# Seven products of sums in place of eight for the logits and gates of a two-layer mixer

## The chip, the cores and the metric

One core of one Trainium2 chip runs the whole network as one program. TensorE (PE) multiplies, VectorE (DVE), ScalarE (ACT) and GpSimd (POOL) do the element work, and all transfers are issued from SyncE's queue (SP). The metric is the device time of one execution in microseconds (us). The kernel before takes 1518.46 us, the median of three runs (the lowest is 1518.29).

## The reference, cut to what matters

Two layers; 512 latent tokens and 256 context tokens, 1024 channels. In each layer the normalised input h goes through one wide input projection, three branches (retention, gMLP, differential attention) make 512 channels each, and the branches are merged by gates that are sigmoids of further columns of the same projection:

```python
def merge_branches(o_ret, o_mlp, o_diff, merge_logits, w_bo, w_o):
    g_ret, g_mlp, g_diff = jnp.split(jax.nn.sigmoid(merge_logits), N_BRANCH, axis=-1)
    y = g_ret * (o_ret @ w_bo[0]) + g_mlp * (o_mlp @ w_bo[1]) + g_diff * (o_diff @ w_bo[2])
    return y @ w_o

# in each layer, with h the modulated, normalised stream (latents, and in layer 0 the context too):
rk_, rv_, dk_, dv_, rq_, rg_, dq_, dg_, mu_, mv_, mg_, mlog_ = split_cols(h @ w_in[l], IN_SIZES)
o_ret  = from_heads(rms_norm(ret_o)) * jax.nn.silu(rg_)
o_diff = from_heads(rms_norm(diff_o) * (1.0 - lam_init)) * jax.nn.silu(dg_)
o_mlp  = mu_ * spatial_mix(layer_norm(mv_)) * jax.nn.silu(mg_)
out = merge_branches(o_ret, o_mlp, o_diff, mlog_, w_branch_out[l], w_out[l])
```

mlog_ has 3072 columns (1024 for each branch), each of the gates and of mu_, mv_ has 512. All is in float32.

## The kernel before, in words

**Precision.** A float32 product is made of three products in TensorE's reduced type: x = xh + xl and w = wh + wl, and wh·xh + wh·xl + wl·xh is accumulated. xh is a copy by ScalarE into the reduced type, xl is x − xh by VectorE; such a pair of instructions is called a split here (`w_split`, L642, for 512 words of weights at a time; `split_into` for activations). h lies split in SBUF through a whole layer (`HH`, `HL`, eight blocks of 128 channels by up to 768 tokens).

**Weights.** They come from HBM in blocks, in the order of `block_list` (L33), through two raw buffers of 2048 words for each partition, and are split into one of two places (`RING`): while one block is multiplied, the next is split. A logit block `m` holds 128 columns of the logits and 128 columns of the branch's output projection.

**A layer** (`run`, L1775): the projections of attention and retention with both branches' own work woven in; then, for the attention branch, the gate `dg` and the merge `d`; for retention the gate `rg` and the merge `r`; then the gMLP (mv, its layer norm, mg, the position mixing and mu) and the merge `m`; then the output phase with the norm and, in layer 0, the next layer's h. In the gates and merges the weights are TensorE's stationary operand (128 columns) and h streams through: 384 tokens at a time in layer 0 (two spans of 768), 512 in layer 1 (latents alone). For 256 columns that is 2 x 2 x 8 x 3 = 96 matmuls 384 wide in layer 0, and 2 x 8 x 3 = 48 matmuls 512 wide in layer 1. The merge (L1477) adds a logit block and an output block for each 128 channels of y: a sigmoid by ScalarE, a multiplication by VectorE, and an addition to y, by GpSimd in the second merge (`ptt`, L1506) and by VectorE in the third.

**Beside it**, in the merges `r` and `m` of layer 0, VectorE computes the modulation of the next layer and the output gate of this one: 32 rows of `wmod`, each loaded by a transfer into one of two buffers and reduced by one or two `ttr` instructions of 1024 elements (L374, in the profile CUSTOM_DVE_ANT_0 with a short read of its accumulator), 56 in all. They write their unused product into the weights' place (`mjunk`).

**What sets the order.** The program records its operations; each has its priority (its place in the recording, moved by a `bump`). `schedule` (L404) then lays them out by a list of assumed costs (L304 to L401), each engine taking the ready operation of lowest priority number. Its result is only an order: on the chip each engine works through its own queue in that order and waits by semaphores. Nearly every instruction comes from one of a few helper lines: L314 matmuls, L318 transposes, L339 ScalarE, L351 tensor_tensor on VectorE, L374 ttr, L392 tensor_tensor on GpSimd, L401 transfers.

Of the kernel before, what the change touches and what calls it, by code (L numbers as in the profile page):

```python
# [568 lines left out]
NR = 32768  # L569


class Prog:
    def __init__(self, nc, R, AR, AFl, PSM, ap):
# [32 lines left out]
    def F(self, *shape):  # L606
# [843 lines left out]

    def gate(self, l, c):
# [3 lines left out]
        oz = Z if c == "d" else Z + 6144  # L1455
        self.OT = self.arv(Z + 3072, 4, NT), self.arv(Z + 9216, 4, NT)
        for i in range(2):
            self.begin(l, f"{c}g{i}")
            W = self.W(l, f"{c}g{i}")
            for j in range(2):  # L1460
                ch = 2 * i + j
                R.tag = f"L{l}.{c}g{ch}"
# [4 lines left out]
                for v, a, b in self.spans(l):
                    R.act(sg[:, a:b], ps[v].ap, AF.Sigmoid)
                for v, a, b in self.spans(l):
                    R.tt(sg[:, a:b], ps[v].ap, sg[:, a:b], ALU.mult)  # L1470
# [4 lines left out]
                self.step()

    def merge(self, l, c, extra=None):  # L1477
# [9 lines left out]
        for i in range(8):  # L1487
            self.begin(l, f"{c}m{i}")
            R.tag = f"L{l}.{c}m{i}"
            Wl = self.W(l, f"{c}m{i}", 128)  # L1490
            Wb = self.W(l, f"{c}m{i}", 128, 1024, 4)
            ps, pb = self.banks(l), self.banks(l)
            sg = F(n)
            y = self.Y[i]
            dst = y if first else sg
            for v, a, b in reversed(self.spans(l)):
                R.tag = f"L{l}.{c}m{i}"
                self.ws(ps[v].ap, (self.HH, self.HL), slice(a, b), Wl, 0)
                self.ws(pb[v].ap, self.OT, slice(a, b), Wb, 0)
                R.tag += ".ev"  # L1500
                R.act(sg[:, a:b], ps[v].ap, AF.Sigmoid)
                R.tt(dst[:, a:b], pb[v].ap, sg[:, a:b], ALU.mult)
                if last:
                    R.tt(y[:, a:b], y[:, a:b], sg[:, a:b], ALU.add)
                    if v == len(self.spans(l)) - 1:
                        self.y_split(l, 0, i)  # L1506
            if not first and not last:
                R.ptt(y.ap, y.ap, sg.ap, ALU.add)
            sg.free()
            for p in (*ps, *pb):  # L1510
                p.free()
            if extra:
                extra(i)
            self.step()
# [374 lines left out]
```

## Time and profile before

| | us |
|---|---|
| median of three runs | 1518.46 |
| the profiled execution | 1517.34 |
| its span, first to last instruction | 1515.5 |
| PE busy | 1493.6 (99%) |
| DVE busy | 797.2 (53%) |
| ACT busy | 600.3 (40%) |
| POOL busy | 170.4 (11%) |

The profiled execution is 1.8 us longer than its span and 1.1 us below the median. Busy time counts an instruction from its start to its end; instructions of one engine that follow each other overlap by some tens of ns, so a row's mean is longer than the distance from one start to the next, and the distance is what a full queue pays. Lines named "windows" give the busy time of each engine in a stretch of the span.

### The profile page before, as it was taken

Reading aid. Unit: us, or ns where it says so; the run is one execution under the profiler, and the core shown is the slowest. Engines: PE = TensorE matmul, PEld = TensorE weight load, DVE = VectorE, ACT = ScalarE, POOL = GpSimd, SP = SyncE. Lnnn points to the kernel's source line nnn. Section 1 sums busy time; section 2 is a strip of 40 time slices with the busy share of each in tenths; the row PEclk is TensorE's granted clock in tenths of the full one; section 3 lists DMA queues with packets and bytes.
Section 4 is the critical chain, followed back from the end, with each engine's and each line's share of the span. In section 5 each row is a group of like instructions: output and inputs, shape, how many; then the busy total and the mean of one; then the engine's idle time right before and its main releaser. Section 6 shows DMA issues by size and latency. Waiting matters only on the chain.

```text
span 1515.5 us, 22649 instructions
## 1 busy us (share of the span) xinstructions
PE 1493.6 (99%) x9040; PEld 1372.6 (91%) x9040; DVE 797.2 (53%) x1551; ACT 600.3 (40%) x1292; POOL 170.4 (11%) x187
## 2 busy tenths in 40 slices
PE   6999999999999999999999999999999999999998
PEld 4789998999999999999999899989998888888887
DVE  4456646565233962335974664674656334344462
ACT  6635644563222222222223462554455333332341
POOL 1211111210000011001000130111211000201000
PEclk9999999999999999999999999999999999999999
DMA  9351322111231532032663233332211332321331
GB/s 362 137 154 36 87 71 60 57 64 45 86 113 56 177 129 84 29 105 76 193 210 125 84 115 92 118 84 84 84 42 57 117 106 84 125 95 62 122 125 70
DMA packets 37705, 156.25 MB, mean 103 GB/s; under 512 B 5344, under 2 KB 6496, under 8 KB 31200
## 3 DMA queue, kind: packets, MB, share of 16 engines
q1 hardware_dynamic: 37600, 154.81, 30.8%
q8 instruction: 71, 1.16, 0.3%
q14 instruction: 34, 0.28, 0.1%
HBM read 132.77 MB, written 4.19 MB: 90 GB/s over the span
## 4 chain that ended last, share of the span: by engine, by line
PE 94%; DVE 2%; issue 1%; DMA 1%; POOL 1%; ACT 0%; SPq 0%; DVEq 0%; POOLq 0%; ACTq 0%
PE PSM L314 91%; PE PSM L318 3%; POOL AF L392 1%; DVE AR L351 0%; ACT AF L339 0%; DVE AF L351 0%; DMA AF<-AF 0%; SPq L401 0%; DMA AF<-w 0%; DVE AF L360 0%; DVE AF L370 0%; DVE AF L366 0%; ACT AR L339 0%; DVEq L1885 0%; POOLq L1885 0%
## 5 line engine op out<-in xcount | busy, mean ns | idle before, releaser
L314 PE MATMUL PSM<-AR 128*128 128x384 f32 (+2 forms) x7512 | 1354.5, 339 | 0.7 <-DVE AF L351 0.7
L314 PEld LDWEIGHTS PSM<-AR 128*128 128x128 f32 x7512 | 1208.5, 189 | 100.9 <-issue 1.2
L339 ACT ACTIVATE AR<-AF 128x512 fp32r<-128x512 f32 (+4 forms) x489 | 284.4, 606 | 414.4 <-PE PSM L314 274.7
L351 DVE TENSOR_TENSOR AR<-AF,AR 128x512 fp32r<-128x512 f32 (+3 forms) x486 | 316.5, 668 | 231.1 <-ACT AR L339 193.3
L392 POOL TENSOR_TENSOR AF<-AF 128x128 f32<-128x128 f32 (+5 forms) x180 | 169.7, 951 | 1340.0 <-DVE AF L351 533.0
L339 ACT ACTIVATE AF<-PSM 128x256 f32<-128x256 f32 (+5 forms) x379 | 169.9, 467 | 356.4 <-PE PSM L314 321.3
L351 DVE TENSOR_TENSOR AF<-PSM,AF 128x512 f32<-128x512 f32 (+3 forms) x253 | 144.8, 581 | 256.2 <-PE PSM L314 160.4
L314 PE MATMUL PSM<-AF 128*128 128x128 f32 (+3 forms) x1104 | 142.0, 300 | 11.8 <-DMA AF<-wmodn 9.6
L314 PEld LDWEIGHTS PSM<-AF 128*128 128x128 f32 (+1 forms) x1104 | 127.0, 184 | 21.3 <-DVE AF L360 9.4
L339 ACT ACTIVATE AF<-PSM,AF 128x768 f32<-128x768 f32 (+2 forms) x144 | 90.9, 646 | 77.8 <-DVE AF L358 48.3
L370 DVE TENSOR_REDUCE AF<-PSM 128x2 f32<-128x1536 f32 (+1 forms) x40 | 61.6, 1542 | 35.7 <-PE PSM L314 35.6
L374 DVE CUSTOM_DVE_ANT_0 AR<-AF 128x1024 fp32r<-128x1024 f32 x59 | 75.3, 1277 | 6.5 <-DMA AF<-wmod 6.1
L360 DVE TENSOR_SCALAR AF<-AF 128x1 f32<-128x1 f32 (+3 forms) x188 | 42.8, 237 | 56.9 <-ACT AF L339 48.8
L318 PE MATMUL PSM<-AF 128*128 128x128 f32 x424 | 67.7, 277 | 3.2 <-ACT AF L339 3.2
L339 ACT ACTIVATE AF<-AF 128x256 f32<-128x256 f32 (+4 forms) x107 | 54.5, 557 | 32.8 <-POOL AF L392 13.4
L318 PEld LDWEIGHTS PSM<-AF 128*128 128x128 f32 x424 | 51.1, 141 | 14.2 <-ACT AF L339 6.4
L351 DVE TENSOR_TENSOR AF<-AF 128x512 f32<-128x512 f32 (+5 forms) x78 | 43.1, 561 | 14.8 <-POOL AF L392 6.0
L366 DVE SCALAR_TENSOR_TENSOR AF<-AF 128x768 f32<-128x768 f32 (+2 forms) x48 | 42.8, 900 | 3.8 <-POOL AF L392 2.7
L382 DVE BATCH_NORM_STATS2 AF<-AF 128x6 f32<-128x512 f32 x10 | 6.7, 691 | 37.6 <-ACT AF L339 37.5
L366 DVE SCALAR_TENSOR_TENSOR AF<-AF,PSM 128x128 f32<-128x128 f32 x64 | 19.9, 344 | 12.4 <-PE PSM L314 6.1
L358 DVE TENSOR_SCALAR AF<-AF 128x2 f32<-128x2 f32 (+4 forms) x98 | 22.1, 239 | 3.2 <-ACT AF L339 1.7
L360 DVE TENSOR_SCALAR AF<-PSM,AF 128x128 f32<-128x128 f32 x48 | 15.8, 403 | 11.4 <-PE PSM L318 11.4
(20 smaller groups left out, 97.9 us busy)
## 6 DMA issues: line engine op xcount, KB each, us to landing
AF<-w SPq DMA_DIRECT2D x50, 1024.0 KB, 4.8
AF<-w SPq DMA_DIRECT2D x48, 768.0 KB, 4.3
AF<-wmod SPq DMA_DIRECT2D x32, 512.0 KB, 4.1
AF<-wmodn SPq DMA_DIRECT2D x16, 512.0 KB, 8.9
AF<-x SPq DMA_DIRECT2D x12, 512.0 KB, 4.4
AR<-AR SPq DMA_DIRECT2D x16, 384.0 KB, 4.3
AF<-AF SPq DMA_DIRECT2D x64, 64.0 KB, 2.0
AR<-AF SPq DMA_DIRECT2D x12, 256.0 KB, 2.3
```

Source lines behind the costliest of these rows:

```text
L314: self.add("PE", lambda: pe.matmul(out, lhsT, rhs, start=start, stop=stop), [out], [lhsT, rhs], c)
L318: self.add("PE", lambda: pe.transpose(out, in_, ident), [out], [in_, ident], 109.0)
L339: return self.add("ACT", lambda: e.activation(out, in_, func, **kw), outs, ins, c, tab)
L351: return self.add("DVE", lambda: v.tensor_tensor(out, a, b, op=op), [out], [a, b], self.n(out) / 0.97 + 84)
L358: f = lambda: v.tensor_scalar(out, a, s1, None, op0=op0)
L360: f = lambda: v.tensor_scalar(out, a, s1, s2, op0=op0, op1=op1)
L366: return self.add("DVE", lambda: v.scalar_tensor_tensor(out, a, s, b, op0=op0, op1=op1), [out], ins, self.n(out) / 0.97 + 130)
L370: return self.add("DVE", lambda: v.tensor_reduce(out, in_, axis=AX.X, op=op), [out], [in_], self.n(in_) / 0.96 + 72)
L374: return self.add("DVE", lambda: v.tensor_tensor_reduce(junk, a, b, 1.0, 0.0, ALU.mult, ALU.add, accum), [junk, accum], [a, b], self.n(a) ...
L382: return self.add("DVE", lambda: v.bn_stats(out, in_), [out], [in_], self.n(in_) / 0.96 + 72)
L392: return self.add("POOL", lambda: g.tensor_tensor(out, a, b, op=op), [out], [a, b], c)
```

## The change

The 256-column products of the logits (`dl`, `rl`, `ml`, four each) and of the gates are no longer made of eight products of quarters (two halves of the channels, two of the columns, two of the tokens) but of seven products of sums of quarters (`seven`). In layer 0 this holds for the logits, rg, mg and mu, 18 products; in layer 1 for the logits, mg and mu, 16. dg, and rg in layer 1, remain eight (`SEVEN`).

- Four sums of quarters of h are made once in a layer and split (`sums`, `sums_split`): S1 = h10 + h11, S2 = S1 − h00, S3 = h00 − h10, S4 = h01 − S2 (first index the half of the tokens, second the half of the channels). S2 and S1 are split after dg, S3 and S4 after mv, whose weights lie in S3's place.
- Four sums of quarters of the weights are made for each product, in the raw buffer, and each of the seven quarters is split (`p_split`): 512 words, into one of five slots of 1024 words (`NSLOT`), which the quarters and the pieces of the output blocks use in turn. A slot is written again when TensorE has read it.
- Each product of quarters is 4 x 3 = 12 matmuls, 384 wide in layer 0 and 256 in layer 1, into a bank of its own. Eight instructions on the results (a copy by ScalarE and seven additions by VectorE, with PSUM as one input) put the four quarters of the result together in SBUF; the sigmoid then reads SBUF.
- The logits and the output projection have blocks of their own (`l` 2048 words, `b` 1024), so a merge goes through four pairs of 256 columns. y is added up a span at a time.
- mv and the layer norm come right after dg (`mlp_v`); mg, mu and the mixing stay ahead of the third merge. The retention's normalised output goes through a DRAM buffer (`scr2`) and comes back when rg is computed; before it lay in SBUF, where S1 is now. `wo0` and `wo1` change places, and y's first group is split in new places.
- The 56 ttr now start in the merge `d` (`MODS`: 8 rows there, 12 in `r`, 12 in `m`), with a priority number raised by 100, and write their product into the upper half of the second raw buffer.

```diff
-    for g in "dr":
-        out += [(f"{g}g{i}", 2048) for i in range(2)] + [(f"{g}m{n}", 1536) for n in range(8)]
-    out += [(f"mv{i}", 2048) for i in range(2)] + [(f"mg{i}", 2048) for i in range(2)] + [(f"mu{i}", 2048) for i in range(2)]
-    out += [(f"mm{n}", 1536) for n in range(8)]
+    for g in ("dg", "mv", "d", "rg", "r", "mg", "mu", "m"):
+        if len(g) == 2:
+            out += [(f"{g}{i}", 2048) for i in range(2)]
+        else:
+            out += [x for i in range(4) for x in ((f"{g}l{i}", 2048), (f"{g}b{i}", 1024))]
...
+MODS = [2, 1, 1, 2, 1, 1, 0, 0], [2, 2, 2, 2, 2, 2, 0, 0], [2, 2, 2, 2, 2, 2, 0, 0]
+SEVEN = ({"dl", "rl", "ml", "mg", "rg", "mu"}, {"dl", "rl", "ml", "mg", "mu"})
+NSLOT = 5
+SLOTS = (Z + 6144, Z, RING[0] + 1024 * NSLOT, None)
...
+    def p_split(self, q):
+        if q >= len(self.pieces) or q in self.pw:
+            return
+        i, x = self.pieces[q]
+        l, name, w, off = self.seq[i]
+        self.w_dma(i)
+        if x == 0:
+            self.w_dma(i + 1)
+        R, raw = self.R, self.raws[i]
+        o = RING[0] + 1024 * ((q - self.pidx[self.idx[l, "mb3"], 1] + 3) % NSLOT)
+        R.bump = PBUMP
+        if name[:2] in SEVEN[l]:
+            b = raw.ap.rearrange("p (a k m n) -> p a m k n", a=2, k=4, m=2)
+            b11, b12, b21, b22 = b[:, 0, 0], b[:, 0, 1], b[:, 1, 0], b[:, 1, 1]
+            t2 = self.T2.ap
+            if x == 2:
+                R.tt(b11, b12, b11, ALU.subtract)
+                R.tt(t2, b22, b11, ALU.subtract)
+            elif x == 4:
+                R.tt(b12, b22, b12, ALU.subtract)
+            elif x == 5:
+                R.tt(b21, b21, t2, ALU.subtract)
+            f = (b11, b21, t2, b11, b12, b21, b22)[x]
+            hi, lo = self.arv(o, 4, 128), self.arv(o + 512, 4, 128)
+        else:
+            f = raw[:, 512 * x:512 * x + 512].rearrange("p (k n) -> p k n", k=2)
+            hi, lo = self.arv(o, 2, 256), self.arv(o + 512, 2, 256)
+        self.split(hi, lo, f)
+        R.bump = 0
+        self.pw[q] = hi, lo
+        if x == (6 if name[:2] in SEVEN[l] else w // 512 - 1):
+            self.w_dma(i + 2)
...
     def mod_item(self, l, n, v, b):
+        self.R.bump = MBUMP
         self.R.ttr(self.mjunk.ap, b.ap, self.silu[v].ap, self.MC[l][:, n, v:v + 1])
+        self.R.bump = 0
...
-        self.mjunk = _View(self.arv(RING[0] + 3072, DM))
+        self.mjunk = _View(self.raw[1][:, 1024:2048])
...
+        def p(x, A):
+            wh, wl = self.pw[self.ahead(l, name, x)]
+            ps = self.P(n)
+            with R.pe():
+                for k in range(4):
+                    a, b = A[0][:, k], A[1][:, k]
+                    R.mm(ps.ap, wh[:, k], a, k == 0, False)
+                    R.mm(ps.ap, wh[:, k], b, False, False)
+                    R.mm(ps.ap, wl[:, k], a, False, k == 3)
+            return ps
...
+        u = F(n)
+        ps = p(0, self.halves(0, 0))
+        R.copy_a(u.ap, ps.ap)
+        c = F(n)
+        ps = p(1, self.halves(0, 1))
+        add(c, ps, u)
+        give(0, 0, c)
+        ps = p(2, S2)
+        add(u, ps, u)
+        p5 = p(3, S1)
+        c12 = F(n)
+        add(c12, p5, u)
+        ps = p(4, S3)
+        add(u, ps, u)
+        c = F(n)
+        add(c, p5, u)
+        give(1, 1, c)
+        ps = p(5, self.halves(1, 1))
+        add(u, ps, u)
+        give(0, 1, u)
+        ps = p(6, S4)
+        add(c12, ps, c12)
+        give(1, 0, c12)
...
-            self.merge(l, "d")
-            self.gate(l, "r")
+            if SEVEN[l]:
+                self.sums(l)
+                self.sums_split(l, (1, 0))
+            self.mlp_v(l)
+            if SEVEN[l]:
+                self.sums_split(l, (2, 3))
+                self.T2 = self.At(512, 4, 128)
...
+            self.merge(l, "d", lambda i: extra(i, MODS[0][i]))
+            self.gate(l, "r")
+            self.merge(l, "r", lambda i: extra(i, MODS[1][i]))
```

**How the order moves.** The new lines shift the helpers by two (L353 is tensor_tensor on VectorE, L376 the ttr, which the order names ISA, L394 tensor_tensor on GpSimd). VectorE's queue in the second merge of layer 0, where GpSimd adds to y (AR is the reduced type, so AR<-AF,AR of 512 is the split of weights; AF<-PSM,AF takes a result of TensorE), before:

```order
L351 TENSOR_TENSOR AF<-PSM,AF 128x384
L374 ISA AR,AF<-AF 128x1024
L374 ISA AF 128x1
L360 TENSOR_SCALAR AF<-AF 128x2
L374 ISA AR,AF<-AF 128x1024
L374 ISA AF 128x1
L351 TENSOR_TENSOR AR<-AF,AR 128x512 x3
L351 TENSOR_TENSOR AF<-PSM,AF 128x384
```

and at the same place now:

```order
L353 TENSOR_TENSOR AF<-PSM,AF 128x384 x3
L376 ISA AF<-AF 128x1024
L376 ISA AF 128x1
L353 TENSOR_TENSOR AR<-AF,AR 128x512 x2
L353 TENSOR_TENSOR AF<-PSM,AF 128x384 x2
L353 TENSOR_TENSOR AR<-AF,AR 128x512
L353 TENSOR_TENSOR AF<-PSM,AF 128x384 x3
L353 TENSOR_TENSOR AR<-AF,AR 128x512
L376 ISA AF<-AF 128x1024
L376 ISA AF 128x1
L353 TENSOR_TENSOR AR<-AF,AR 128x512
```

The splits are now of single quarters, each between additions of results, and a ttr stands among them.

GpSimd's queue from the last work of the retention to the first work of layer 0's output, before (the eight additions to y of the second merge, the norm's root, the four products of the gMLP):

```order
L392 TENSOR_TENSOR AF<-AF 128x4
L392 TENSOR_TENSOR AF<-AF 128x2
L392 TENSOR_TENSOR AF<-AF 128x768 x8
L392 TENSOR_TENSOR AF<-AF 128x6
L392 TENSOR_TENSOR AF<-AF 128x768 x4
```

and now:

```order
L394 TENSOR_TENSOR AF<-AF 128x4
L394 TENSOR_TENSOR AF<-AF 128x2
L394 TENSOR_TENSOR AF<-AF 128x6
L394 TENSOR_TENSOR AF<-AF 128x384 x16
L394 TENSOR_TENSOR AF<-AF 128x768 x4
```

The norm's root (128x6) is ahead of the merges, and the additions are half as wide and twice as many.

VectorE's queue in the gMLP of layer 1 (gates mg), before:

```order
L360 TENSOR_SCALAR AF<-AF 128x512 x4
L351 TENSOR_TENSOR AF<-PSM,AF 128x512
L351 TENSOR_TENSOR AR<-AF,AR 128x512 x4
L351 TENSOR_TENSOR AF<-PSM,AF 128x512 x2
L351 TENSOR_TENSOR AR<-AF,AR 128x512 x4
```

and now (128x4x128 and 128x512 from AF to AF are the sums of weight quarters):

```order
L353 TENSOR_TENSOR AR<-AF,AR 128x512
L353 TENSOR_TENSOR AF<-AF 128x4x128
L353 TENSOR_TENSOR AF<-PSM,AF 128x256
L353 TENSOR_TENSOR AR<-AF,AR 128x512
L353 TENSOR_TENSOR AF<-AF 128x512
L353 TENSOR_TENSOR AF<-AF 128x4x128 x2
L353 TENSOR_TENSOR AR<-AF,AR 128x512 x2
L353 TENSOR_TENSOR AF<-PSM,AF 128x256 x2
```

Sums of weights and additions of results have joined the splits between one product's quarters and the next's.

More of the change, by code (lines that the diff above doesn't have):

```diff
@@ L562 @@
 WBUMP = -20
+PBUMP = -60
+MBUMP = 100
+SBUMP = 60
+CBUMP = -100
 ABUMP = -100
@@ L588, in __init__ @@
         self.idx = {(l, n): i for i, (l, n, w, o) in enumerate(self.seq)}
+        self.pieces = []
+        for i, (l, name, w, off) in enumerate(self.seq):
+            j = i % len(BLOCKS)
+            if SEVEN[l] and self.idx[0, "dl0"] <= j < self.idx[0, "wo0"]:
+                self.pieces += [(i, x) for x in range(7 if name[:2] in SEVEN[l] else w // 512)]
+        self.pidx = {x: q for q, x in enumerate(self.pieces)}
+        self.pw = {}
         self.side = [], []
@@ new lines, in sums_split @@
+    def sums_split(self, l, js):
+        R = self.R
+        n = self.half(l)
+        R.tag = f"L{l}.sums"
+        R.bump = PBUMP
+        for j in js:
+            o = SLOTS[j]
+            if o:
+                hi, lo = self.arv(o, 4, n), self.arv(o + 4 * n, 4, n)
+            else:
+                hi, lo = self.halves(1, 0) if l == 0 else (self.arv(x + 8 * n, 4, n) for x in SLOTS[:2])
+            for k in (slice(0, 2), slice(2, 4)):
+                self.split(hi[:, k], lo[:, k], self.S4[j][:, k])
+            self.S4[j].free()
+            self.SX[j] = hi, lo
+        R.bump = 0
@@ L1451, in gate, with product @@
+    def product(self, l, name, done):
+        (self.seven if name[:2] in SEVEN[l] else self.eight)(l, name, done)
     def gate(self, l, c):
@@ L1486, in merge @@
                 self.Y.append(Buf(self.fm, self.AFl, o, n, (n,)))
[L1487 to L1514, printed above, removed]
@@ L1517, in mlp, with done @@
-    def mlp(self, l):
+        for p in range(4):
+            G = {}
+            def done(m, a, b, ps):
+                if m not in G:
+                    G[m] = F(n)
+                R.act(G[m][:, a:b], ps, AF.Sigmoid)
+            self.product(l, f"{c}l{p}", done)
+            name = f"{c}b{p}"
+            end = last and p == 3
+            if end:
+                self.ahead(l, name)
+                self.T2.free()
+                self.w_split(self.idx[l, "wo0"])
+                for i in range(6):
+                    R.tag = f"L{l}.ysp0"
+                    self.y_split(l, 0, i)
+            if SEVEN[l]:
+                q = self.ahead(l, name)
+                W = [[x[:, k] for x in self.pw[q + e]] for e in range(2) for k in range(2)]
+            else:
+                self.begin(l, name)
+                hi, lo = self.W(l, name, 256, 0, 4)
+                W = [(hi[:, k], lo[:, k]) for k in range(4)]
+            for m in range(2):
+                i = 2 * p + m
+                y = self.Y[i]
+                for v, a, b in self.spans(l) if l == 0 or not end else ((0, 0, 256), (1, 256, 512)):
+                    R.tag = f"L{l}.{name}"
+                    pb = self.P(b - a)
+                    with R.pe():
+                        for k in range(4):
+                            wh, wl = (x[:, 128 * m:128 * m + 128] for x in W[k])
+                            xh, xl = (x[:, k, a:b] for x in self.OT)
+                            R.mm(pb.ap, wh, xh, k == 0, False)
+                            R.mm(pb.ap, wh, xl, False, False)
+                            R.mm(pb.ap, wl, xh, False, k == 3)
+                    R.tag += ".ev"
+                    g = G[m][:, a:b]
+                    R.tt(y[:, a:b] if first else g, pb.ap, g, ALU.mult)
+                    pb.free()
+                    if last:
+                        R.tt(y[:, a:b], y[:, a:b], g, ALU.add)
+                    elif not first:
+                        R.ptt(y[:, a:b], y[:, a:b], g, ALU.add)
+                G[m].free()
+                if end:
+                    R.tag = f"L{l}.ysp0"
+                    self.y_split(l, 0, i)
+                if extra:
+                    extra(i)
+                self.step()
@@ L1597, in mlp, with done @@
-        for b in [wst, bs, *vn]:
+                sil[g].free()
+            def done(j, a, b, ps):
+                f = sp[j][:, a:b]
+                R.tt(f, ps, f, ALU.mult)
+                self.split(self.OT[0][:, 2 * i + j, a:b], self.OT[1][:, 2 * i + j, a:b], f)
+            self.product(l, f"mu{i}", done)
+            for j in range(2):
+                sp[j].free()
+        for b in [wst, bs, self.vb]:
             b.free()
```

257 lines of the change are left out of this document (175 added, 82 removed).

## The prediction

> **What bounds the kernel now.** I read the page's first two parts first, then the chain of waits, the busy time by stage, and last the rows of PE, DVE and POOL in order of time. The page and the chain:
>
> ```profile
> PE 1493.6 (99%) x9040; PEld 1372.6 (91%) x9040; DVE 797.2 (53%) x1551; ACT 600.3 (40%) x1292; POOL 170.4 (11%) x187
> PEclk9999999999999999999999999999999999999999
> PE 94%; DVE 2%; issue 1%; DMA 1%; POOL 1%; ACT 0%; SPq 0%; DVEq 0%; POOLq 0%; ACTq 0%
> 371.49 473.65 PE PSM L314 x2768
> ```
>
> PE works all the time at the full clock, and all that the change touches in layer 0 is one unbroken piece of 473.65 us in which PE waits for nobody. A matmul less is its time less, until something else comes late. What could is in the windows (span, us; then busy us of PE, PEld, DVE, ACT, POOL):
>
> ```profile
> core 0: us, PE busy (x) PEld busy (x) DVE busy (x) ACT busy (x) POOL busy (x), PEclk, DMA share, GB/s
> 98.00:371.00 273.00, 271.59 (x1942) 256.47 (x1943) 164.97 (x352) 140.73 (x364) 45.43 (x54) 1.00 0.21 65
> 538.00:640.00 102.00, 102.00 (x593) 98.55 (x592) 35.89 (x61) 22.63 (x43) 13.36 (x6) 1.00 0.22 77
> 740.00:788.00 48.00, 48.00 (x279) 48.00 (x278) 38.70 (x84) 12.02 (x23) 0.00 (x0) 1.00 0.68 222
> 1280.00:1372.00 92.00, 92.00 (x452) 78.14 (x452) 34.76 (x58) 28.48 (x50) 12.54 (x8) 1.00 0.29 103
> ```
>
> In layer 0's second merge (538 to 640) DVE has two thirds of its time free, in layer 1's (1280 to 1372) the same. In the third (740 to 788) the ttr fill it to 81%.
>
> **What the matmuls lose.** PE's rows in order of time (start, length, count) give the distance of one matmul to the next, from the start of a row to the start of the next:
>
> ```profile
> 705.29 83.45 PE L314 MATMUL PSM<-AR 128*128 128x384 f32 x480
> 788.58 1.05 PE L314 MATMUL PSM<-AF 128*128 128x128 f32 x8
> 1391.91 54.67 PE L314 MATMUL PSM<-AR 128*128 128x512 f32 x240
> 1446.42 1.06 PE L314 MATMUL PSM<-AF 128*128 128x128 f32 x8
> 891.49 8.87 PE L314 MATMUL PSM<-AR 128*128 128x256 f32 x72
> 900.20 1.04 PE L318 MATMUL PSM<-AF 128*128 128x128 f32 x8
> ```
>
> 384 wide: 83.29/480 = 0.1735 us. 512 wide: 54.51/240 = 0.2271. 256 wide: 8.71/72 = 0.1210, which is more than half of 0.2271.
>
> - Layer 0, each of 18 products: 96 before, 84 now, 12 x 0.1735 = 2.08 us less; together 37.5.
> - Layer 1, each of 16: 48 x 0.2271 = 10.90 before, 84 x 0.1210 = 10.16 now, 0.74 less; together 11.8.
> - The last output block of layer 1 is split at 256: 48 x 0.1210 for 24 x 0.2271, 0.4 more.
>
> That is 48.9 us less, and 1517.3 − 48.9 = 1468.4 if PE still waits for nobody. Most of it is layer 0's; in layer 1 the narrower matmuls eat half of the eighth that is saved. The bound above for 256 wide is half the 512's, 0.1135: then layer 1 saves 10 us more.
>
> [...]
>
> **What DVE gains.** Its rows in layer 0's second merge, and three groups by form (busy, mean ns):
>
> ```profile
> 545.75 0.69 DVE L351 TENSOR_TENSOR AR<-AF,AR 128x512 fp32r<-128x512 f32 x1
> 546.35 1.22 DVE L374 CUSTOM_DVE_ANT_0 AR<-AF 128x1024 fp32r<-128x1024 f32 x1
> 547.50 0.69 DVE L351 TENSOR_TENSOR AR<-AF,AR 128x512 fp32r<-128x512 f32 x1
> 549.25 0.55 DVE L351 TENSOR_TENSOR AF<-PSM,AF 128x384 f32<-128x384 f32 x1
> 549.72 0.68 DVE L351 TENSOR_TENSOR AR<-AF,AR 128x512 fp32r<-128x512 f32 x1
> 550.31 2.87 DVE L374 CUSTOM_DVE_ANT_0 AR<-AF 128x1024 fp32r<-128x1024 f32 x1
> 553.12 0.08 DVE L374 DVE_READ_ACCUMULATOR2_ANT AF<- 128x1 f32 x1
> ...
> L351 DVE TENSOR_TENSOR AF<-PSM,AF 128x256 f32<-128x256 f32 x42 | 16.9, 421 | 37.9 <-ACT AF L339 21.5 <-PE PSM L314 14.5 <-POOL AF L392 1.8
> L351 DVE TENSOR_TENSOR AR<-AF,AR 128x768 fp32r<-128x768 f32 x12 | 11.5, 957 | 3.5 <-ACT AR L339 3.4
> L339 ACT ACTIVATE AR<-AF 128x512 fp32r<-128x512 f32 x356 | 216.3, 628 | 311.7 <-PE PSM L314 274.7 <-DVE AF L351 26.8 <-DMA AF<-w 5.4
> ```
>
> By the starts, a 512 costs the queue 0.60 us (545.75 to 546.35), a 384 0.47, a ttr 1.15. By the same 0.09 off the mean, a 256 costs 0.33 and a 768 0.87.
>
> One product of seven is 7 splits and 4 weight sums of 512 and 7 additions. Layer 0: 11 x 0.60 + 7 x 0.47 = 9.9 us against 84 x 0.1735 = 14.6 of PE. Layer 1: 11 x 0.60 + 7 x 0.33 = 8.9 against 10.2. An output block adds 2 x 0.60 + 4 x 0.47 = 3.1 against 8.3 in layer 0, 2.4 against 5.45 in layer 1. So a merge has 52 us of DVE in 91.6 of PE, or 45 in 62. ACT has 7 splits of 0.63 and five smaller ones, 7 us at most, in each product, and stays free.
>
> Then, where DVE is short:
>
> - Layer 0's rg: 2 x (9.9 + 12 x 0.47) = 31.1 against 29.1, 2 over.
> - Its second merge: 52 + 24 ttr of 1.15 = 79.6 against 91.6. But GpSimd adds here, and that costs DVE time. The ttr of 550.31 above took 2.87 instead of 1.22, until GpSimd was done:
>
> ```profile
> 549.88 2.23 POOL L392 TENSOR_TENSOR AF<-AF 128x768 f32<-128x768 f32 x1 [11.99 <-DVE AF L351]
> 687.95 1.84 POOL L392 TENSOR_TENSOR AF<-AF 128x768 f32<-128x768 f32 x1 [8.11 <-DVE AF L351]
> L392 POOL TENSOR_TENSOR AF<-AF 128x512 f32<-128x512 f32 x36 | 50.7, 1408 | 322.5 <-DVE AF L351 183.8 <-DMA AF<-AF 105.0 <-PE PSM L314 19.1
> ```
>
>   A 768 is 1.84 us alone, a 512 1.4, so a 384 some 1.1, and 16 of them may hold DVE for 17.6: 97.2 in all, 5.6 over. In the trace such a hold costs nothing, since DVE has time; now it has none.
> - Its mg: 23.6 against 29.1. mu: 2 x (9.9 + 12 x 0.47) = 31.1, and four GpSimd products of 1.84, 38.5 against 29.1 and 24 small matmuls, 31.6: 6.9 over. Ahead of it DVE can gain only what five slots hold, 5 x 0.94 = 4.7 us with the weight sums.
>
> That makes 2 + 5.6 + 6.9 − 4.7, about 10 us that PE waits in layer 0. The small matmuls by
>
> ```profile
> 675.06 1.50 PE L314 MATMUL PSM<-AF 128*128 128x128 f32 x12
> 676.31 8.57 PE L314 MATMUL PSM<-AR 128*128 128x384 f32 x48
> ```
>
> at 1.25/12. Layer 1's second merge takes its eight adds of 1.4 (45 + 11 in 62). Its mg has 20.4 against 20.3; mu 2 x (8.9 + 1.2 + 2.6) + 4 x 1.4 = 31 against 22: 9 over, less 4.7, 4.5.
>
> **The rest of the change.**
>
> - The sums of h: 28 instructions of 0.87 (layer 0) or 0.60, 24 and 17 us of DVE beside dg and mv, 67 and 44 us of PE. Only S3 and S4 must wait for mv's last matmul, 3.5 or 2.4 us in the first product, which has 4.7 and 1.3 free. Between nothing and 4 each; I take 2 each, 4.
> - The end of the third merge: four splits of wo0 (0.60) and six of y (256 wide, 0.33), 4.4 us, and the last output block's own 1.2 + 8 x 0.47 = 5.0 in layer 0, 1.2 + 8 x 0.33 = 3.8 in layer 1, against 8.3 and 5.8 of PE. Over by 1 and 2.4; nothing if wo0 is split late, I take 3 for both.
> - mv's move costs nothing by itself: the same matmuls, and its weights' two transfers move with it in SP's queue.
> - Transfers:
>
> ```profile
> AF<-w SPq DMA_DIRECT2D x50, 1024.0 KB, 4.8
> AF<-wmod SPq DMA_DIRECT2D x32, 512.0 KB, 4.1
> AR<-AR SPq DMA_DIRECT2D x16, 384.0 KB, 4.3
> AR<-AF SPq DMA_DIRECT2D x12, 256.0 KB, 2.3
> ```
>
>   The bytes of weights are the same. A logit's weights can be fetched only when the last quarter before them is split; then comes an output block, 5.45 us of PE in layer 1, and the fetch (4.8) and the first split (1.3) take 6.1: one quarter's lead (1.45 of PE) hides it, and without that it is 0.7 at each of nine places in layer 1, 6 in all. The retention's output goes out as before and comes back by eight loads, four of 384 KB; SP issues them while PE is in the output block ahead, and unhidden they cost 4.3 each. In raw buffer two a transfer of 2048 words waits for the ttr ahead of it, and on SP all that stands behind it waits too; rg1 is the one such place with ttr ahead of it, one whole product early.
>
> Sum: 1468.4 + 10 + 4.5 + 4 + 3 = 1490. The median of the runs shown stands 1 us above the profiled time.
>
> **Rivals.** *The cover holds* (35%): GpSimd's holds fall where DVE has a result to add or waits anyway, and ttr slip into gaps, so only starts and ends are left: 1468 + 7 = 1475. For it: between 98 and 371 PE is busy 271.59 of 273 beside chains through all engines. Against it: the counts above leave no gap in mu.
>
> *DVE pays its full recorded lengths* (7%), 0.69, 0.55, 0.42 and 1.22, as it would if each instruction waited for the one before it to end. Layer 0's product is then 11.4 and layer 1's 10.5, above PE's 10.2; rg is 7 over, the second merge 15, mu 12, layer 1's gMLP 18, starts and ends 9, 61 in all: 1529. Against it are the starts above, 0.60 apart. [...]
>
> *The ring runs dry* (5%), slower: an output block needs both its slots to its end, so three quarters at most are ready at the next product's start. If DVE, in order, stands at a split that waits for a slot while the additions that free a bank are behind it, quarters are made in the open, 0.63 + 0.69 = 1.32 us each. Of 294 quarters and pieces 37 (one in eight) use up the gain and 60 (one in five) make it 2% slower; two in each of 34 products give 1468 + 90 = 1558. Against it: ACT and DVE are free for most of each output block.
>
> *Narrow matmuls* (3%): 0.13 instead of 0.121 beside busy engines would cost 84 x 16 x 0.009 = 12, 1502.
>
> **The numbers.** My forecast, DVE held by GpSimd and over in rg and mu, has 50%, from 1482 to 1503 by its own. About 2% is what a measurement of this kernel can tell from no change; 2% below 1518.5 is 1488, and a quarter of the forecast's cases lies below it. Faster: 35 + 12 = 47%. Slower: the dry ring and a little, 6%. Within 2%: 47%. The range from 1466 to 1512 holds the forecast, the first rival and the narrow matmuls, and leaves out the other two and the tails.
>
> **What would show it.** Right: matmuls down by 216 of 384 wide; in layer 0's second merge and in mu DVE near full with PE busy below 95%, splits or ttr above 1.3 us beside GpSimd's rows, and PE full in the first and third merges. The first rival: PE at 99% in all windows. The dry ring: PE waits for DVE or ACT at each product's fourth quarter, in all merges. I am wrong if PE's waits lie at transfers or in the projections ahead of dg, where nothing should change.

## The result, and the profile after

The changed kernel takes 1477.69 us, the median of four runs (1477.43 to 1477.89), against 1518.75 for the kernel before beside it: a ratio of 0.9731, 95% interval 0.9711 to 0.975, so 2.7% faster. One of the four runs of the kernel before took 3272.58 us and is left out of the ratio. The profiled execution took 1477.75 us with a span of 1476.0. The forecast was 1490 in a range from 1466 to 1512: the sign of the difference was right, its size was 28 us forecast and 41 measured. The matmuls came out as forecast; what was too large is the forecast of waits, 21.5 us, where some 9 were found.

The page's busy line, the granted clock and the engines' shares of the chain:

```profile
PE 1448.1 (98%) x9424; PEld 1354.4 (92%) x9424; DVE 1086.6 (74%) x2119; ACT 689.6 (47%) x1488; POOL 173.6 (12%) x195
PEclk9999999999999999999999999999999999999999
PE 83%; DVE 9%; issue 3%; DMA 2%; ACT 2%; POOL 1%; SPq 1%; DVEq 0%; POOLq 0%; ACTq 0%
```

The chain of waits in order of time (start, length, what), its two longest pieces:

```profile
376.62 166.46 PE PSM L316 x959
547.64 188.71 PE PSM L316 x1104
```

TensorE still works 98% of the time at the full clock. VectorE went from 53% to 74% and joined the chain with 9%. All of layer 0's gates and merges up to 736 us are, but for 0.4 us at 547, two pieces in which TensorE waits for nobody.

The busy time by stage (span; then PE, PEld, DVE, ACT, POOL) in layer 0's second merge, its third, layer 1's second merge, its gMLP, and layer 1's projections and attention; and that last stage in the kernel before, in the second fence:

```profile
core 0: us, PE busy (x) PEld busy (x) DVE busy (x) ACT busy (x) POOL busy (x), PEclk, DMA share, GB/s
545.00:629.00 84.00, 83.76 (x483) 83.44 (x482) 83.93 (x146) 30.37 (x56) 22.70 (x16) 1.00 0.36 126
697.00:740.00 43.00, 43.00 (x250) 43.00 (x250) 42.26 (x84) 16.25 (x28) 0.00 (x0) 1.00 0.38 137
1255.00:1315.00 60.00, 60.00 (x416) 56.17 (x416) 50.91 (x85) 27.51 (x55) 10.27 (x8) 1.00 0.33 119
1340.00:1370.00 30.00, 26.75 (x217) 25.85 (x216) 30.00 (x64) 13.39 (x28) 4.57 (x3) 1.00 0.33 122
966.00:1138.00 172.00, 170.35 (x1174) 156.49 (x1173) 115.01 (x219) 88.54 (x208) 26.42 (x31) 1.00 0.24 78
```

```profile
1006.00:1178.00 172.00, 172.00 (x1182) 158.90 (x1181) 104.23 (x207) 86.85 (x204) 25.02 (x31) 1.00 0.23 72
```

In layer 0's second merge VectorE is busy 83.93 of 84 us, and TensorE waits only 0.24. In layer 1's gMLP VectorE is busy all the time too, and there TensorE does wait. Layer 1's attention, whose matmuls the change leaves alone, lost 1.65 us of TensorE.

The matmuls, from the rows of PE by form and in order of time. The kernel before had 2496 that are 384 wide, 2600 of 512 and 2416 of 256:

```profile
L316 PE MATMUL PSM<-AR 128*128 128x256 f32 x3808 | 482.0, 284 | 3.7 <-DVE AF L353 3.3 <-DVE AR L353 0.4
L316 PE MATMUL PSM<-AR 128*128 128x512 f32 x1808 | 443.2, 395 | 0.7 <-DVE AF L353 0.7
L316 PE MATMUL PSM<-AR 128*128 128x384 f32 x2280 | 401.1, 335 | 0.2 <-ACT AF L341 0.2
```

```profile
654.36 14.81 PE L316 MATMUL PSM<-AR 128*128 128x384 f32 x84
669.01 2.84 PE L316 MATMUL PSM<-AF 128*128 128x128 f32 x24
...
1333.80 10.32 PE L316 MATMUL PSM<-AR 128*128 128x256 f32 x84
1343.95 1.95 PE L316 MATMUL PSM<-AF 128*128 128x128 f32 x16
1345.65 1.67 PE L316 MATMUL PSM<-AR 128*128 128x256 f32 x12
1348.40 1.66 PE L316 MATMUL PSM<-AR 128*128 128x256 f32 x12 [1.08 <-DVE AF L353]
1350.27 8.87 PE L316 MATMUL PSM<-AR 128*128 128x256 f32 x72 [0.21 <-DVE AF L353]
1360.17 3.13 PE L316 MATMUL PSM<-AR 128*128 128x256 f32 x24 [1.04 <-DVE AF L353]
1363.70 1.67 PE L316 MATMUL PSM<-AR 128*128 128x256 f32 x12 [0.40 <-DVE AF L353]
```

216 of 384 are gone, and a product of 84 takes 14.65/84 = 0.1744 us for each; in layer 1 10.15/84 = 0.1208. Both distances are within 1% of those of before. So TensorE lost the 48.9 us of the sum, and since the execution became 39.6 shorter (1517.34 − 1477.75), new waits took back 9.3. To place them, each distance from one matmul's start to the next is compared with the usual one of its width, and what it has above that is counted as a wait. Less what the kernel before has by the same count, they lie here: about 4.0 in layer 1's gMLP and the first product of the third merge behind it (the last rows above), 2.8 in layer 1's attention, 1.6 ahead of dg, 0.9 in layer 0's gates and merges (0.41 at 547, 0.45 at 760), 0.6 at the end of layer 1's third merge; together 9.9, which agrees with 9.3 as closely as this way of counting can.

### The profile page after: what moved, and what is told of

It is laid out like the page before. It is cut to its first block, busy times and chain, and to the rows that moved or that the text cites. A ratio compares the mean times of both kernels' runs of the same rounds, so it can differ in the third digit from the quotient of the medians.

```text
span 1476.0 us, 24501 instructions
## 1 busy us (share of the span) xinstructions
PE 1448.1 (98%) x9424; PEld 1354.4 (92%) x9424; DVE 1086.6 (74%) x2119; ACT 689.6 (47%) x1488; POOL 173.6 (12%) x195
## 4 chain that ended last, share of the span: by engine, by line
PE 83%; DVE 9%; issue 3%; DMA 2%; ACT 2%; POOL 1%; SPq 1%; DVEq 0%; POOLq 0%; ACTq 0%
PE PSM L316 79%; DVE AR L353 3%; DVE AF L353 3%; PE PSM L320 3%; DMA AF<-w 1%; POOL AF L394 1%; ACT AF L341 1%; DVE AF L372 1%; SPq L403 1%; ACT AR L341 1%; DMA AF<-x 0%; DVE AF L362 0%; DVE AF L368 0%; DVE AF L376 0%; DVE AF L360 0%
## 5 line engine op out<-in xcount | busy, mean ns | idle before, releaser
L316 PE MATMUL PSM<-AR 128*128 128x256 f32 (+2 forms) x7896 | 1305.4, 324 | 4.6 <-DVE AF L353 3.9
L341 ACT ACTIVATE AR<-AF 128x512 fp32r<-128x512 f32 (+5 forms) x623 | 356.6, 601 | 340.7 <-PE PSM L316 174.6
L353 DVE TENSOR_TENSOR AR<-AF,AR 128x512 fp32r<-128x512 f32 (+4 forms) x620 | 407.5, 681 | 72.3 <-ACT AR L341 67.1
L353 DVE TENSOR_TENSOR AF<-PSM,AF 128x384 f32<-128x384 f32 (+3 forms) x461 | 237.2, 530 | 126.7 <-PE PSM L316 66.9
L394 POOL TENSOR_TENSOR AF<-AF 128x128 f32<-128x128 f32 (+7 forms) x188 | 172.9, 932 | 1297.4 <-DVE AF L353 452.5
L341 ACT ACTIVATE AF<-PSM 128x256 f32<-128x256 f32 (+5 forms) x321 | 137.5, 448 | 201.4 <-PE PSM L316 170.4
L353 DVE TENSOR_TENSOR AF<-AF 128x512 f32<-128x512 f32 (+6 forms) x268 | 160.5, 622 | 15.5 <-PE PSM L316 4.2
L341 ACT ACTIVATE AF<-AF 128x256 f32<-128x256 f32 (+5 forms) x227 | 110.2, 512 | 122.0 <-DVE AF L353 104.4
L316 PE MATMUL PSM<-AF 128*128 128x128 f32 (+3 forms) x1104 | 142.8, 304 | 11.8 <-DMA AF<-wmodn 9.1
L376 DVE CUSTOM_DVE_ANT_0 AF<-AF 128x1024 f32<-128x1024 f32 (+1 forms) x60 | 72.8, 1213 | 0.0
L353 DVE TENSOR_TENSOR AF<-AF,AR 128x512 f32<-128x512 f32 (+2 forms) x40 | 29.8, 766 | 0.6 <-PE PSM L316 0.5
```

Source lines behind the costliest of these rows:

```text
L316: self.add("PE", lambda: pe.matmul(out, lhsT, rhs, start=start, stop=stop), [out], [lhsT, rhs], c)
L341: return self.add("ACT", lambda: e.activation(out, in_, func, **kw), outs, ins, c, tab)
L353: return self.add("DVE", lambda: v.tensor_tensor(out, a, b, op=op), [out], [a, b], self.n(out) / 0.97 + 84)
L376: return self.add("DVE", lambda: v.tensor_tensor_reduce(junk, a, b, 1.0, 0.0, ALU.mult, ALU.add, accum), [junk, accum], [a, b], self.n(a) ...
L394: return self.add("POOL", lambda: g.tensor_tensor(out, a, b, op=op), [out], [a, b], c)
```

## Experiments

### Each layer's sevens alone, and none

`SEVEN` is a table, so a layer can be put back to eight products while the ring of quarters, the sums of h, mv's move and the output through DRAM stay:

```diff
-SEVEN = ({"dl", "rl", "ml", "mg", "rg", "mu"}, {"dl", "rl", "ml", "mg", "mu"})
+SEVEN = ({"dl", "rl", "ml", "mg", "rg", "mu"}, {"none"})      # x2
+SEVEN = ({"none"}, {"dl", "rl", "ml", "mg", "mu"})            # x3
+SEVEN = ({"none"}, {"none"})                                  # x5
```

In x3 and x5 layer 0's eight products read S4 where a quarter of h lay, so they compute with a changed h; the instructions are those of eight products.

> Layer 1's logits and gates are made of eight products again (quarters of the weights, the ring and the sums of h stay). By the prediction's sum 11.8 us of TensorE and 0.4 for nothing come back, and its own waits (gMLP 4, end 0.6) go: 1477.7 + 11.8 - 4.6 = 1485. Rival, that the narrow matmuls and VectorE's work eat what the seven save in layer 1: 1478 or less.

> Layer 0's logits and gates are made of eight products again, the ring, the sums and the order of the branches stay. By the prediction's sum 18 x 12 x 0.1735 = 37.5 us come back and less than 1 us of waits goes: 1514 to 1515. Rival, that seven products cost layer 0 hidden waits (10 us, as forecast): 1505.

> No product is made of seven; the ring of quarters, the sums of h, mv's move, the output through DRAM and the new places of the ttr stay. If the gains of the two layers are what the runs with one layer alone gave, and independent, 1477.7 + 8.2 + 37.1 = 1523, so all the rest of the change costs 4 to 5 us against before. If the rest costs nothing, 1518.5, and the two layers' gains overlap.

Measured: 1485.86 us with layer 0 alone (ratio to before 0.9785, 0.977 to 0.98), 1514.88 with layer 1 alone (0.9981, 0.9971 to 0.9991), 1525.08 with neither (1.0041, 1.0026 to 1.0056). Layer 0's sevens are worth 1514.88 − 1477.69 = 37.2 us on top of layer 1's, and the sum had 37.5; the ten runs of x3 spread from 1511.91 to 1518.96, so this is known to about 1.5 us. Layer 1's are worth 8.2, against 11.8 less the 4.5 of its gMLP, 7.3. Without either, the rest of the change costs 1525.08 − 1517.81 = 7.3 us against the kernel before beside it. By the distances from start to start nearly all of it is waits: 1.7 more at the program's start, 1.2 at the first product of layer 0's merges, 2.0 in layer 1's attention, the rest in small pieces.

VectorE in layer 0's second merge, with eight products:

```profile
545.00:640.00 95.00, 95.00 (x550) 95.00 (x549) 50.38 (x88) 24.27 (x45) 16.54 (x13) 1.00 0.33 114
```

It is busy 53% here, 100% with seven: the sevens took an eighth of TensorE's matmuls off these products and paid with the whole of VectorE's free time.

### GpSimd's holds

In x1 VectorE does GpSimd's additions to y and its products in the gMLP; in x8 GpSimd does each addition of layer 0 three times, and VectorE's queue stays the same.

```diff
-                        R.ptt(y[:, a:b], y[:, a:b], g, ALU.add)
+                        R.tt(y[:, a:b], y[:, a:b], g, ALU.add)          # x1
-                R.ptt(f.ap, f.ap, sil[g].ap, ALU.mult)
+                R.tt(f.ap, f.ap, sil[g].ap, ALU.mult)                  # x1

+                        for op in (ALU.add, ALU.subtract) if l == 0 else ():   # x8
+                            R.ptt(y[:, a:b], y[:, a:b], g, op)
                         R.ptt(y[:, a:b], y[:, a:b], g, ALU.add)
```

> The 16 + 8 additions to y in the second merges and the eight products of the gMLP go from GpSimd to VectorE; nothing is left out. Holds theory (the prediction's: GpSimd holds VectorE for its whole length): layer 1's gMLP gets back 4 x 1.4 and pays 4 x 0.60, so its wait of 4 us goes to about 1 and the time to 1474.5. Lead theory (each stretch in which VectorE is over lives on the lead it has in the ring of weight quarters, and the holds are short because VectorE mostly reads PSUM or waits then): layer 0 has no wait to lose, VectorE pays 16 x 0.47 there and gets about 5 back; in layer 1 it pays 2.4 and gets about 1 back, so 1478 to 1480.

> In layer 0's second merge GpSimd adds each piece to y, takes it away and adds it again: 48 instructions in place of 16; VectorE's queue is the same, word for word. Full holds, as forecast (1.1 us of VectorE for each): 35 us more, less some 8.5 of lead and free time, 1504. Partial holds (0.3 us each, as the longer rows of the second merge add up to 4.9 for 16): 10 us more, 1478 to 1480.

x1 took 1478.4 us (1476.95 to 1479.77), as the changed kernel and as the lead theory had it (1478 to 1480). x8 took 1491.74, 14.0 longer: between the two expectations, near to neither. VectorE's rows by form between 545 and 629 (busy, mean ns), in the changed kernel, in x1 and in x8:

```profile
L376 DVE CUSTOM_DVE_ANT_0 AF<-AF 128x1024 f32<-128x1024 f32 x21 | 29.3, 1393 | 0.0
L353 DVE TENSOR_TENSOR AR<-AF,AR 128x512 fp32r<-128x512 f32 x32 | 24.3, 774 | 0.0
L353 DVE TENSOR_TENSOR AF<-PSM,AF 128x384 f32<-128x384 f32 x45 | 23.2, 546 | 0.0
L353 DVE TENSOR_TENSOR AF<-AF 128x4 f32<-128x4 f32 x4 | 2.2, 563 | 0.0
```

```profile
L376 DVE CUSTOM_DVE_ANT_0 AF<-AF 128x1024 f32<-128x1024 f32 x20 | 24.3, 1217 | 0.0
L353 DVE TENSOR_TENSOR AF<-PSM,AF 128x384 f32<-128x384 f32 x45 | 23.9, 552 | 1.8 <-PE PSM L316 1.3 <-ACT AF L341 0.2
L353 DVE TENSOR_TENSOR AR<-AF,AR 128x512 fp32r<-128x512 f32 x32 | 21.5, 686 | 1.1 <-ACT AR L341 1.0
```

```profile
L376 DVE CUSTOM_DVE_ANT_0 AF<-AF 128x1024 f32<-128x1024 f32 x21 | 34.0, 1620 | 0.0
L353 DVE TENSOR_TENSOR AR<-AF,AR 128x512 fp32r<-128x512 f32 x25 | 27.8, 1124 | 0.0
L353 DVE TENSOR_TENSOR AF<-PSM,AF 128x384 f32<-128x384 f32 x36 | 18.6, 545 | 0.0
```

and GpSimd's own rows there, in the changed kernel and in x8:

```profile
L394 POOL TENSOR_TENSOR AF<-AF 128x384 f32<-128x384 f32 x16 | 22.7, 1442 | 181.3 <-DVE AF L353 181.3
```

```profile
L394 POOL TENSOR_TENSOR AF<-AF 128x384 f32<-128x384 f32 x36 | 58.1, 1642 | 146.4 <-DVE AF L353 142.5 <-PE PSM L316 3.4
```

Against x1, where GpSimd does nothing, the 16 additions make 21 ttr 0.176 us longer and 32 splits 0.088, 3.7 + 2.8 = 6.5 us, 0.41 for each addition. The four short instructions of the norm (128x4) add 4 x 0.41 = 1.6, since they take 0.15 in x1, where they stand behind the merge; together some 8.1, 0.5 for each addition. In x8 the first two groups alone make 21 x 0.403 + 25 x 0.438 = 19.4 for 36 additions, 0.54 each. The forecast took 1.1. The additions that read PSUM take 0.55 in all three (546, 552 and 545 ns), also in x8, where GpSimd is busy 58.1 of the 84 us: they are not held at all. So in these rows the long ones have both inputs in SBUF (the ttr with 1.39 against 1.22, the splits with 0.77 against 0.69, the norm's 128x4 with 0.56 against 0.15), and one input from PSUM goes with the usual length; the rows do not show why. The sums of weights have two SBUF inputs too and are not longer here (682 ns, 685 in x1), because by the rows in order of time none of them runs beside an addition of GpSimd; three that do in x8 take 1.03 to 1.38. One row with a single tensor input is held all the same, a tensor_scalar of two columns at 621.94 with 0.52 us, where the one at 621.26 takes 0.22. GpSimd pays as well: its first addition takes 1.02, the mean is 1.44, and 1.64 in x8.

So the holds were there, at about half of their price. What paid for them was a second thing, VectorE's lead: how long ahead of TensorE's first matmul of an output block its first split is done, by both queues in order of time. At the four output blocks of layer 0's second merge:

```
changed kernel   6.6  5.3  4.2  3.5 us
x1               6.6  6.3  6.8  6.8
x8               6.6  4.0 -1.5 -1.4
x10 (four slots) 4.9  3.0  2.3  0.9
```

VectorE starts this merge 6.6 us ahead and falls behind by 3 in it; the smallest lead is 1.6, at a quarter of the fourth logit block. The holds are larger than this loss. x1 keeps its lead, but it does not isolate them: there VectorE has 16 additions more, 16 x 0.47 = 7.5 us, and some of its ttr and the norm's short instructions stand later. x8 does, since there the queue is the same: the lead is used up in the third block, and TensorE waits at one split after the other, always at the third matmul of a quarter or piece, the first that reads the part that VectorE makes (PE in order of time):

```profile
589.29 2.36 PE L316 MATMUL PSM<-AR 128*128 128x384 f32 x12 [0.32 <-DVE AR L353]
592.65 2.36 PE L316 MATMUL PSM<-AR 128*128 128x384 f32 x12 [1.00 <-DVE AR L353]
596.01 1.33 PE L316 MATMUL PSM<-AR 128*128 128x384 f32 x6 [1.00 <-DVE AR L353]
599.36 15.36 PE L316 MATMUL PSM<-AR 128*128 128x384 f32 x78 [2.02 <-DVE AR L353]
```

The same waits added up from 523 to 632 (us in total, times, longest):

```profile
PE PSM L316 <- DVE AR L353: 8.3, 8, 2.0
```

The rest of the 14.0 is told in the last section.

### How full VectorE is

The ttr of layer 0's second merge are done twice, half of them (x6) or all (x7):

```diff
-        self.R.ttr(self.mjunk.ap, b.ap, self.silu[v].ap, self.MC[l][:, n, v:v + 1])
+        for _ in range(1 + (self.twice and v == 0)):     # x7: 1 + self.twice
+            self.R.ttr(self.mjunk.ap, b.ap, self.silu[v].ap, self.MC[l][:, n, v:v + 1])
```

> 12 of the 24 ttr of layer 0's second merge are done twice, 12 x 1.15 = 13.8 us more for VectorE there. Lead theory (VectorE is full there and lives on what it is ahead of TensorE, some 3 us by the end of this merge, and on the 5.5 it has free in mg): 13.8 - 8.5, about 5 us longer, 1483. Filler theory (the 99% is ttr that fill time which VectorE has free): 1477 to 1479.

> All 24 ttr of layer 0's second merge are done twice, 27.6 us more for VectorE there. Lead theory: 27.6 - 8.5 = 19, 1497, so from 12 to 24 more the time rises by nearly all of their 13.8. Filler theory: below 1480.

Measured: 1494.31 and 1507.35, that is 16.6 and 29.6 longer. That the added ttr cost nothing, as the filler theory had it, is out. From 12 to 24 more the time rises by 13.0 for 13.8 us of ttr, as expected in size. But the first 12 should have cost 5 and cost 16.6. PE in order of time in x6:

```profile
624.80 5.02 PE L316 MATMUL PSM<-AR 128*128 128x384 f32 x28
630.50 8.25 PE L316 MATMUL PSM<-AR 128*128 128x384 f32 x46 [0.69 <-DVE AR L353]
646.63 1.65 PE L316 MATMUL PSM<-AF 128*128 128x128 f32 x6 [7.87 <-DVE AF L353]
653.38 11.91 PE L316 MATMUL PSM<-AR 128*128 128x384 f32 x53 [5.10 <-ACT AR L341]
```

and its chain of waits at that place:

```profile
646.57 1.15 DVE AF L376 x2
...
647.74 4.87 DMA AF<-w
...
652.70 0.64 ACT AR L341
```

The planner put the added ttr together into mg, and they write their unused product into the second raw buffer. The weights for the next product could be fetched there only when the last ttr was done: 4.87 us of transfer in the open, and 7.9 us before it in which VectorE's ttr held up what TensorE needed. These waits, 13.7 us with the 0.69, are not all of the 16.6: from 653.4 to 658.5 TensorE works at a granted clock of 0.50, which costs some 2.6 more (the 53 matmuls behind 653.38 take 11.91 us, at 0.1744 each 9.2; the last section has more on this). In x7 the same place makes one wait of 19.93 us, which ends with the same transfer (4.79), so its 13.0 are ttr in a row in front of a transfer and no measure of the lead. And VectorE itself stands idle for 2.32 us at 617.8 in x6, for ScalarE's part of a split. So this pair of runs shows neither how much lead VectorE keeps nor, by itself, that it has no time left; for that there are the 83.93 of 84 us. The raw buffer is a second cause that I had not taken apart.

### A shorter ring

```diff
-NSLOT = 5
+NSLOT = 4
```

> The ring has four slots in place of five, so VectorE can be one quarter less ahead: 2.08 us in layer 0, 1.45 in layer 1. Lead theory: in layer 0's second merge, where the lead falls to 3.5 at the last output block and 1.6 at a quarter ahead of it, and in layer 1's gMLP, waits grow by about that, 2 to 4 us in all: 1480 to 1482. If the ring's depth is not what covers these stretches: 1478. If the ring runs dry at each of 34 products, as the rival of the prediction had it: 1500 and more.

1483.97 us, the runs spread from 1480.34 (the profiled one) to 1485.05; the ratio to before is 0.9765 (0.9751 to 0.978), and 0.9724 (0.971 to 0.9739) for the changed kernel beside it. The profiled run is what the lead theory gives, 1480 to 1482; the median is 2 us more, 7.0 above the changed kernel beside it. The lead in layer 0 is 1.7 to 2.5 shorter at each block of the table above, and still no new wait comes there. Layer 1's second merge, without a wait before, has them now:

```profile
1255.00:1315.00 60.00, 57.96 (x391) 53.15 (x391) 48.47 (x81) 26.06 (x52) 9.61 (x6) 1.00 0.33 121
```

It waits there at splits, 2.5 us in four places. In layer 1's gMLP, where more waits were expected too, there are fewer: 1.1 us from 1340 to 1372 against 3.3 in the changed kernel. That 34 products run dry is out even with four slots.

### Layer 1's gMLP

x4 makes mg and mu of layer 1 of eight products, x9 mu alone; x12 is x9 with the four products of layer 1's gMLP on VectorE; x11 is the changed kernel once more.

```diff
-SEVEN = (..., {"dl", "rl", "ml", "mg", "mu"})
+SEVEN = (..., {"dl", "rl", "ml"})            # x4
+SEVEN = (..., {"dl", "rl", "ml", "mg"})      # x9
...
+                (R.ptt if l == 0 else R.tt)(f.ap, f.ap, sil[g].ap, ALU.mult)   # x12, and x9's table
```

> Only mg and mu of layer 1 are made of eight products again. 4 x 0.74 = 3.0 us of TensorE come back; if the 4 us of waits there are VectorE's overload by the seven, they go: 1476.7. If they come from GpSimd's products or the small matmuls, which stay, 1480.7.

> Only mu of layer 1 is made of eight products, mg stays seven. 2 x 0.74 = 1.5 us come back. If mu alone made the wait of 4 us (as forecast: mg 20.4 against 20.3, mu 9 over), all of it goes: 1475.2. If mg shares in it, 1 to 2 us of wait stay and the time is that of the run with both made of eight, 1476.3, or above.

> As the run with mu of layer 1 made of eight products, and its four products on GpSimd go to VectorE: 4 x 0.60 more for VectorE, four holds and rows of 1.4 less. If no wait is left there, the same as without it, 1475.2; if holds leave one, up to 1 us below.

> The changed kernel itself, for a comparison on the same chip: 1477.7.

Measured: 1476.34, 1475.92, 1475.33 and 1476.93, with runs of one kernel up to 2.6 us apart. The times can't be told apart from each other; only x4's rival, 1480.7, is out. The profiles can be: the same stage in x9,

```profile
1325.00:1370.00 45.00, 45.00 (x290) 41.02 (x289) 37.66 (x67) 19.67 (x39) 5.77 (x4) 1.00 0.31 106
```

TensorE waits nowhere in it, and VectorE has 16% free. So mu's seven products were the overload. What ran out, though, was not the ring. All five waits of the changed kernel stand at the first matmul of a quarter, which writes into a bank of PSUM, and end with an instruction of VectorE that reads PSUM and so empties one (AF<-PSM, `DVE AF` in the rows of PE), where x8's and x10's end with a split (`DVE AR`). VectorE's rows around the first of them, which ends at 1348.40:

```profile
1347.85 0.41 DVE L353 TENSOR_TENSOR AF<-PSM,AF 128x256 f32<-128x256 f32 x1
1348.18 0.68 DVE L353 TENSOR_TENSOR AR<-AF,AR 128x512 fp32r<-128x512 f32 x1
1348.78 1.67 DVE L353 TENSOR_TENSOR AF<-PSM,AF 128x256 f32<-128x256 f32 x4
```

So VectorE was late in emptying banks, not in filling slots. This would also be why four slots wait less here: VectorE can't go so far ahead with splits, so its additions may come earlier; no run shows that. The sevens of mu save nothing in layer 1: 1.5 us of matmuls for 4 of waits, of which x1, with GpSimd's products on VectorE, still had 2.7 by the same count. A kernel with mu of layer 1 made of eight products is at least as fast as the changed one, by about a microsecond that these runs don't settle.

## Why the prediction was right and where it was not

- **The matmuls: right.** 48.9 us by count and distance; the counts and the two distances came out as they stand, and x3 measured layer 0's part at 37.2, within 1.5.
- **Layer 0's waits, 10 us: wrong, 0.9 measured.** The step that failed is "2 + 5.6 + 6.9 − 4.7". Its three overloads were taken together against one lead. The lead is larger, 6.6 us of TensorE's time at an output block of layer 0 (five slots of which each feeds 2.08 us of matmuls; 4.7 was what VectorE needs to fill them), and each stretch starts with a filled ring: mg, which has VectorE to spare, fills it between the merge and mu. And the second merge's 5.6 rested on holds of 17.6, which measured some 8.1. The three overloads took 0, about 3 (6.6 to 3.5) and about 4 us of lead (from 9.5 at mu's first quarter to 5.1 at the third merge's) and left some each time.
- **VectorE near full with rows above 1.3 us beside GpSimd: right, but TensorE below 95% there: wrong.** 84 us of 84, a mean ttr of 1.39, splits of 0.77, and TensorE at 83.76. Full as it was, VectorE did not delay TensorE there, since it was ahead of it.
- **Layer 1's gMLP, 4.5: right in size, 4.0, and in its cause**, VectorE's overload in mu: x4 and x9 take it away by giving VectorE back its time. The way to the number is luck in part. The sum takes a lead of 4.7 off an overload of 9 (which makes 4.3, not 4.5), and 5.6 of these 9 are GpSimd's holds; without them x1 still has 2.7 of the 4.0, and the waits end at banks that VectorE empties late, which the sum has no term for.
- **Starts, 4: wrong, nothing.** TensorE goes through the first product of each layer's merges without a break. Only with eight products in layer 0 (x3, x5) is there a wait, of 1.2. **Ends, 3: 0.6 measured**, in layer 1, and in the second profile of the same kernel (x11) 0.5 more at the end of layer 0's third merge; layer 0's only wait near there, 0.45 at 760 us, is at small matmuls for the norm's factors (`gp_rows`), which wait for VectorE inside the merge.
- **Waits in the projections ahead of dg**, of which the prediction said that they would make it wrong: 2.8 us in layer 1's attention and 1.6 earlier, nearly half of all new waits, so by its own sign the prediction was wrong in this part. The change records nothing new in them but the transfer to DRAM and, late in layer 1's attention, the first sums, but the planner has laid out layer 1's attention anew on all engines. By the same count, and with nothing taken off, layer 1's attention has 4.1 us in the changed kernel, 1.3 in the kernel before, and 1.9 to 3.9 in x2 to x5. That the new order causes them is argued, not shown; no run put the old order back. The 1.6 is within what the start differs by from run to run.
- **The rivals.** *The cover holds*, 1475, was nearest to the measured time. Its reason is half of the truth: additions that read PSUM are not held (0.55 us beside GpSimd and without it), but the ttr have no gaps to slip into (83.93 of 84 us), and the holds cost some 8.1 us which the lead pays. *Full recorded lengths* (1529) and *the ring runs dry* (1558) are out by the time, *narrow matmuls* by 0.1208.

The sum with the measured terms: 1517.3 − 48.9 + 0.9 + 4.0 + 0.6 + 2.8 + 1.6 = 1478.3, against 1477.75.

## What to carry to other kernels

Where one engine prepares pieces for another through a ring, an overload of so many microseconds is no wait of so many: hold each overloaded stretch against the lead that the ring can store in time of the engine that is fed, and ask whether the stretch between two of them fills it again. Ask too what else the same engine has to clear: in layer 1's gMLP the results that VectorE had to read out of PSUM came late before its splits did. The engine's busy share doesn't tell: at 100% it cost nothing in layer 0 and 4 us in layer 1. Seven products for eight pay where the streams stay wide (37 us at 384 columns) and hardly where they become narrow (8 us at 256), and they take the free time of the engine that adds.

## What the runs showed of the hardware

Waits of TensorE cost more than their length in x8: they add up to 8.3 us, and the time is 14.0 longer. After the waits of 0.3 to 2.0 us shown above, the granted clock fell (the windows' last three columns are the clock, the DMA share and GB/s):

```profile
596.00:599.00 3.00, 1.33 (x6) 1.01 (x6) 3.00 (x4) 0.17 (x1) 2.68 (x2) 1.00 0.55 202
599.00:602.00 3.00, 2.64 (x9) 2.65 (x10) 3.00 (x7) 0.98 (x2) 0.00 (x0) 0.59 0.78 228
602.00:605.00 3.00, 3.00 (x16) 3.00 (x15) 3.00 (x6) 1.16 (x2) 0.00 (x0) 0.84 0.28 111
628.00:631.00 3.00, 2.95 (x9) 2.95 (x10) 3.00 (x6) 0.00 (x0) 0.00 (x0) 0.50 0.14 22
631.00:634.00 3.00, 3.00 (x11) 3.00 (x11) 3.00 (x6) 0.63 (x1) 0.00 (x0) 0.55 0.85 328
```

In narrower windows the clock is 0.50 from 599.6 to 602.8 and from 627.0 to 633.6, and 1.00 right behind 603.1. Between 599 and 605 and between 628 and 634 some 4.6 us went to the slower clock (3 us times what is missing from 1, added up), which with the 8.3 of waits makes 12.9 of the 14.0. In the changed kernel the waits of up to 1.1 us in layer 1's gMLP, each followed by 1.6 us of work or more, left the clock at 1.00 throughout 1340 to 1370. In x8 the longest wait at each of the two slower stretches is 2.02. In x7 one such stretch stands behind a single wait: after 17.0 us of matmuls without a break TensorE waits 2.12 us, to 1458.85, and then has a clock of 0.50 for some 3 us:

```profile
1459.60:1462.80 3.20, 3.20 (x17) 3.20 (x17) 1.36 (x4) 1.89 (x4) 0.00 (x0) 0.50 0.61 225
```

The longer waits shown above have a lower clock about them too: x6's 7.87 and 5.10 us, with 0.57 as the mean from 640 to 660, and x7's 19.93, with 0.68 from 640 to 660 and 0.81 from 660 to 680. Waits of up to 1.13 us in the changed kernel behind its start (at 260) and of 1.16 in x10 (at 1270) left it at 1.00.
